# Hybrid encoder layer on one core: the moving operand of every rounded product read from two places in turn

## The chip, the core and the metric

The kernel runs on one NeuronCore of a Trainium2 chip. The metric is device time in microseconds of one execution; the kernel before takes 2334.44 us (median of three runs, 2333.82 to 2335.02). The profile is of one execution and its times are read as spans and starts on that core. The engines are TensorE (PE, its weight loads shown apart as PEld), VectorE (DVE), ScalarE (ACT), GpSimd (POOL) and the sync engine (SP), which issues most DMA.

## The reference

One layer over 256 tokens of width 2048, in float32:

```
x += 0.5 * post(FFN1(pre(x)))                  # SwiGLU, hidden width 5504
x += post(W_o(g_A * MLA(h) + g_B * RWKV7(h)))  # h = pre(x), one wide input projection w_in
x += post(XAttn(pre(x), mem))                  # cross-attention into 256 memory tokens
x += 0.5 * post(FFN2(pre(x)))
```

Nearly all of the arithmetic is dense products of 256 tokens with weight matrices (about 420 MB of weights). The RWKV scan is done in chunks of 32 tokens, with a small inverse per chunk and head.

## The kernel before, in words

**Split products.** A float32 matrix is written as a high part rounded to the engine's fast format (`float32r`) and a rounded remainder, hi + lo. A product of two such matrices is made of products of rounded parts, accumulated in one PSUM bank. `weights` (L287) streams the weights: tiles of 128 x 1024 arrive by DMA on the SP queue (`wraw`, four buffers), ACT copies the high part (L317, `whi`), DVE subtracts to get the low part (L318, `wlo`), both into rings of three slots. A tile holds 1024/n blocks of 128 x n, where n is the width of the column cut (`_CUTS`, L1579); the host's `_tiles` (L1587) lays the weights out in DRAM in just that order.

**Two forms.** In the *channel form*, `lin_ch_steps` (L330), the weights stand still in the array and the tokens move. The activations lie as high and low halves side by side (`x[:, k]` is 2 x 256 columns), so one product of the high weights with 512 moving columns (L358) and one of the low weights with the 256 high columns (L361) make a step of 128 channels; the two halves of the PSUM tile are then copied (L367) and added (L368) into `half`, and an evacuation takes it from there. The FFN's gate and up projections, the RWKV r and k, the low-rank columns, the memory keys and the cross-attention queries go this way. With `before` (one block of FFN2, L343 and L344) the two token halves are done apart.

In the *token form*, `lin_tok_steps` (L375), the tokens stand still (two blocks of 128) and n weight columns move, with three products for each block k and token half t: hi x hi (L390), hi x lo (L391), lo x hi (L392). PSUM then holds tokens by output columns. The FFN's down projections, the query latent, the RWKV v, the gates, and all output projections go this way, mostly with n = 512, the memory values with 256, the query expansion with 384 and the key/value latent with 320. `mla_heads` (L808) does the key/value expansion by hand, six kinds of products (L825 to L832) with both forms side by side on the same tile.

**What sets the order.** Within a block the code's order is the engine's order. The RWKV scan is woven with other products by `weave` (L258): a generator of the scan's steps yields how many microseconds of other work it wants in between, and a generator of *fill* work is advanced, each step counted at a fixed price, until that is reached. A token-form step (three products) is priced at `TOK_US`, a channel-form step at twice `CH_US` (L36: 0.68 and 0.35). The fill is two blocks of the attention output, the second half of r and k, two more output blocks, and then eight gate blocks of 32 steps, 256 steps in all. The scan's wants from the moment that the gate blocks begin are 2.0; eight times 1.3 (Gram matrices); 59.0 (while DVE inverts the chunk matrices, which go to memory and back into `G` at L1161); 2.2 and 1.4; six times 2.0, 2.2 and 1.4; 2.0 and 2.2; 10.0, 4.0, 6.5 and 3.0; 5.5; 5.0 and 5.0.

Products that take unrounded float32 operands (the attention scores and values, among them L1522 and L1533, the transposes, such as L517, and the scan's small products) are written separately.

Of the kernel before, what the change touches and what calls it, by code (L numbers as in the profile page):

```python
# [18 lines left out]
P = 128  # L19
# [13 lines left out]
BEFORE = 6  # L33
LEAD = 100
FIRST = 1000000
TOK_US, CH_US = 0.68, 0.35  # L36

COLS = {}

# [43 lines left out]
class Passage:  # L83
# [93 lines left out]
class Layer:  # L177
# [109 lines left out]
    def weights(self, w, nk, c0, n, feed=None, still=False, parts=False):  # L287
# [3 lines left out]
        for k in range(0, nk, kt):  # L291
# [11 lines left out]
            for j, stop in zip(cuts, cuts[1:]):  # L303
# [19 lines left out]
                for i in range(j, j + step):  # L323
                    yield k + i, hi[:, i * n : (i + 1) * n], lo[:, i * n : (i + 1) * n]

    def lin_ch(self, *args):
        for _ in self.lin_ch_steps(*args):
            pass

    def lin_ch_steps(self, w, nk, c0, n, x, evac, feed=None, before=0, parts=False, spare=False):  # L330


        nc = self.nc
        nt = n // P
        pool, tag = (self.pst, "tr") if spare else (self.psm, "mm")
        ps = [pool.tile([P, 2, T], F32, tag=tag, name="mm") for _ in range(nt)]
        held = []

        def one(t, k, hi, lo):
            ts = slice(t * P, (t + 1) * P)  # L340
            for j in range(nt):
                s = slice(j * P, (j + 1) * P)
                nc.tensor.matmul(ps[j][:, :, ts], hi[:, s], x[:, k, :, ts], start=(t + k == 0), stop=False)  # L343
                nc.tensor.matmul(ps[j][:, :, ts], lo[:, s], x[:, k, :, ts], start=False, stop=False)  # L344

        for k, hi, lo in self.weights(w, nk, c0, n, feed, True, parts):
            if k < before:
                held.append((k, hi, lo))
                one(0, k, hi, lo)
                yield k  # L350
                if k == before - 1:
                    for h in held:
                        one(1, *h)
                    yield k
                continue
            for j in range(nt):
                s = slice(j * P, (j + 1) * P)
                both = lambda: nc.tensor.matmul(ps[j], hi[:, s], x[:, k], start=(k == 0), stop=(k == nk - 1))  # L358
                if k < nk - 1:
                    both()  # L360
                nc.tensor.matmul(ps[j][:, 0, :], lo[:, s], x[:, k, 0], start=False, stop=False)  # L361
                if k == nk - 1:
                    both()
            yield k
        for j in range(nt):
            y = self.tmp.tile([P, T], F32, tag="half", name="half", bufs=2)
            nc.scalar.copy(out=y, in_=ps[j][:, 1, :])  # L367
            nc.vector.tensor_add(y, y, ps[j][:, 0, :])  # L368
            evac(j, y)

    def lin_tok(self, *args):
# [3 lines left out]
    def lin_tok_steps(self, w, nk, c0, n, xh, xl, evac, skew=0, passage=None, before=0):  # L375

        nc = self.nc  # L380
        if passage is not None:
            extra = (nk - skew + 1) // 2 * 2
            self.extra = {extra: passage.slots[0], extra + 2: passage.slots[1]}
        ps = [self.psm.tile([P, n], F32, tag="mm", name="mm") for _ in range(NT)]

        def part(x, t, k):
            return x[t][:, k, :] if isinstance(x, list) else x[:, k, t * P : (t + 1) * P]

        def step(t, k, hi, lo, first=0, last=nk - 1):
            nc.tensor.matmul(ps[t], part(xh, t, k), hi, start=(k == first), stop=False)  # L390
            nc.tensor.matmul(ps[t], part(xh, t, k), lo, start=False, stop=False)  # L391
            self.last_mm = nc.tensor.matmul(ps[t], part(xl, t, k), hi, start=False, stop=(k == last))  # L392

        held = []
        for k, hi, lo in self.weights(w, nk, c0, n):
            if k < before:
                held.append((k, hi, lo))
                step(0, *held[-1])
                yield k
                if k == before - 1:  # L400
                    for h in held:
                        step(1, *h)
                        yield k
                    held = []
                continue
            if k >= nk - skew:
                if passage is not None and not held:
                    passage.enter()
                held.append((k, hi, lo))
                if passage is not None:  # L410
                    step(0, *held[-1])
                continue
            for t in range(NT):
                step(t, k, hi, lo)
                yield k
        if passage is not None:
# [391 lines left out]
    def mla_heads(self, pool):  # L808
        nc, a = self.nc, self.a
# [5 lines left out]
        for c in range(4):  # L815
            psk = [self.psm.tile([P, T], F32, tag="mm", name="mm") for _ in range(2)]
            psv = [self.psm.tile([P, T], F32, tag="mm", name="mm") for _ in range(2)]
            for k, hi, lo in self.weights(a["w_ukv"], 2, c * 512, 512):
                kh, kl = self.ckh, self.ckl
                hv = hi.rearrange("p (h x c) -> p h x c", h=2, x=2)[:, :, 1, :]  # L820
                lv = lo.rearrange("p (h x c) -> p h x c", h=2, x=2)[:, :, 1, :]
                first, last = k == 0, k == 1
                for j in range(2):
                    s = slice(j * 256, j * 256 + P)
                    nc.tensor.matmul(psk[j], hi[:, s], kh[:, k, :], start=first, stop=False)  # L825
                    nc.tensor.matmul(psk[j], hi[:, s], kl[:, k, :], start=False, stop=False)
                    nc.tensor.matmul(psk[j], lo[:, s], kh[:, k, :], start=False, stop=last)
                for t in range(NT):
                    s = slice(t * P, (t + 1) * P)
                    nc.tensor.matmul(psv[t], kh[:, k, s], hv, start=first, stop=False)  # L830
                    nc.tensor.matmul(psv[t], kh[:, k, s], lv, start=False, stop=False)
                    nc.tensor.matmul(psv[t], kl[:, k, s], hv, start=False, stop=last)  # L832
            for j in range(2):
                nc.scalar.copy(out=self.knT[:, 2 * c + j, :], in_=psk[j])
                nc.scalar.copy(out=self.mv[:, j, c * 256 : (c + 1) * 256], in_=psv[j])
            if c == 1:
                self.do_later()

# [719 lines left out]
def layer(ctx: ExitStack, tc, a):  # L1558
# [28 lines left out]
def _tiles(w, cuts):  # L1587
# [4 lines left out]
    for n in cuts:  # L1592
        kt = WT // n
        for k in range(0, nk, kt):
            out.append(w[k * P : (k + kt) * P, c0 : c0 + n].reshape(-1, P, n).transpose(1, 0, 2).reshape(-1))
        c0 += n
    assert c0 == w.shape[1]
    return np.concatenate(out)


def _layout(inputs):
    f = lambda n: np.ascontiguousarray(np.asarray(inputs[n]))
    arr = {"x": f("x")[0], "mem": f("mem")[0], "positions": f("positions")[0].reshape(NT, P).T}
# [40 lines left out]
```

## Time and profile before

| | |
|---|---|
| median of three runs | 2334.44 us |
| span of the profiled execution | 2333.1 us |
| around the span, against the median | 1.3 us |
| TensorE busy | 2314.2 us |
| VectorE busy | 1465.1 us |
| ScalarE busy | 1136.7 us |
| DMA moved | 449.27 MB, mean 193 GB/s |
| mean granted TensorE clock | 0.998 |

A group's row reads: line, engine, operation, tile written and tiles read, array rows and columns, shape, count, then busy time and the mean duration of one, then the idle time of the engine ahead of it with what ended it. A timeline row reads: start, duration, engine, line, operation. A source row gives the shortest, median and longest duration in ns, then the first and last start. Durations of products overlap: the next one starts while the one before still drains, so the pace is read from starts.

### The profile page before, as it was taken

The numbers are of one execution on the slowest core, as the hardware profiler recorded it, in microseconds if no ns is written. First come the engines' busy times: TensorE is split into PE (matmuls) and PEld (weight loads), VectorE is DVE, ScalarE is ACT, GpSimd is POOL, SyncE is SP. The second block draws the span as 40 slices with busy tenths as digits, with TensorE's granted clock in tenths as the row PEclk, the third lists the DMA queues.
The fourth block names the chain that finished last, engine by engine and source line by source line (L and its number), as shares of the span: only waits on it lengthen the run. The fifth ranks groups of instructions, "written<-read, shape, count | busy, mean of one in ns | idle before, by whom it ended". The sixth has DMA issues, their size and how long they took to land.

```text
span 2333.1 us, 34972 instructions
## 1 busy us (share of the span) xinstructions
PE 2314.2 (99%) x13664; PEld 1984.1 (85%) x13664; DVE 1465.1 (63%) x2137; ACT 1136.7 (49%) x1670; POOL 76.3 (3%) x127
## 2 busy tenths in 40 slices
PE   9999999999999999999999999999999999999997
PEld 8888888888888888888777889888888888888886
DVE  7666666654447677768567766557666666664444
ACT  6445444544446566544334555446544544444442
POOL 0000000000000101000131000000000000000000
PEclk9999999999999999999999999999999999999999
DMA  7655555566666664545657765445555555566664
GB/s 251 208 201 190 189 190 190 189 199 198 198 198 214 210 194 152 166 148 176 212 174 243 267 200 181 169 160 172 188 190 191 190 190 191 190 200 197 198 192 144
DMA packets 137670, 449.27 MB, mean 193 GB/s; under 512 B 24096, under 2 KB 25504, under 8 KB 137248
## 3 DMA queue, kind: packets, MB, share of 16 engines
q1 hardware_dynamic: 131696, 431.94, 56.8%
q0 software_dynamic: 4944, 14.69, 2.0%
q8 instruction: 107, 1.75, 0.3%
q10 hardware_dynamic: 864, 0.40, 0.1%
q14 instruction: 59, 0.48, 0.1%
HBM read 436.48 MB, written 10.49 MB: 192 GB/s over the span
## 4 chain that ended last, share of the span: by engine, by line
PE 94%; issue 2%; DVE 2%; DMA 1%; ACT 1%; POOL 0%; SPq 0%; DVEq 0%; ACTq 0%; POOLq 0%
PE mm L358 31%; PE mm L361 16%; PE mm L390 14%; PE mm L391 14%; PE mm L392 14%; DVE wlo L318 1%; PE gr L1118 0%; PE po L1189 0%; PE po L1233 0%; PE pu L1214 0%; PE tr L494 0%; PE pn L1223 0%; PE po L1204 0%; PE bt L1122 0%; DVE X L600 0%
## 5 line engine op out<-in xcount | busy, mean ns | idle before, releaser
L318 DVE TENSOR_TENSOR wlo<-wraw,whi 128x1024 fp32r<-128x1024 f32 (+3 forms) x792 | 954.4, 1207 | 709.8 <-ACT whi L317 697.1
L317 ACT CAST whi<-wraw 128x1024 fp32r<-128x1024 f32 (+3 forms) x792 | 820.1, 1036 | 881.1 <-PE mm L392 454.8
L358 PE MATMUL mm<-hT,whi 128*128 128x512 f32 x3280 | 1140.0, 394 | 0.5 <-DVE hT L485 0.5
L361 PE MATMUL mm<-hT,wlo 128*128 128x256 f32 x3280 | 909.2, 283 | 0.5 <-DVE wlo L318 0.5
L358 PEld LDWEIGHTS mm<-hT,whi 128*128 128x128 f32 x3280 | 610.5, 188 | 126.2 <-ACT whi L317 0.8
L361 PEld LDWEIGHTS mm<-hT,wlo 128*128 128x128 f32 x3280 | 619.2, 189 | 10.1 <-DVE wlo L318 1.3
L392 PE MATMUL mm<-whi,ml 128*128 128x512 f32 x680 | 264.9, 390 | 0.0
L390 PE MATMUL mm<-whi,mh 128*128 128x512 f32 x680 | 264.8, 389 | 0.0
L391 PE MATMUL mm<-wlo,mh 128*128 128x512 f32 x680 | 264.8, 389 | 0.0
L390 PE MATMUL mm<-whi,hT 128*128 128x512 f32 (+2 forms) x512 | 188.7, 369 | 0.2 <-ACT hT L484 0.2
L391 PE MATMUL mm<-wlo,hT 128*128 128x512 f32 (+2 forms) x512 | 184.7, 361 | 1.7 <-DVE wlo L318 1.7
L392 PE MATMUL mm<-whi,hT 128*128 128x512 f32 (+2 forms) x512 | 183.9, 359 | 0.2 <-DVE hT L485 0.2
L392 PEld LDWEIGHTS mm<-whi,ml 128*128 128x128 f32 x680 | 127.7, 188 | 26.6
L390 PEld LDWEIGHTS mm<-whi,mh 128*128 128x128 f32 x680 | 127.7, 188 | 26.4
L391 PEld LDWEIGHTS mm<-wlo,mh 128*128 128x128 f32 x680 | 127.7, 188 | 26.2
L367 ACT COPY half<-mm 128x256 f32<-128x256 f32 x206 | 75.2, 366 | 134.1 <-PE mm L358 134.1
L368 DVE TENSOR_TENSOR half<-half,mm 128x256 f32<-128x256 f32 x206 | 86.1, 418 | 53.4 <-ACT half L367 53.3
L391 PEld LDWEIGHTS mm<-wlo,hT 128*128 128x128 f32 x512 | 96.4, 188 | 16.4 <-DVE wlo L318 3.3
L390 PEld LDWEIGHTS mm<-whi,hT 128*128 128x128 f32 x512 | 96.3, 188 | 15.8 <-ACT hT L484 0.5
L392 PEld LDWEIGHTS mm<-whi,hT 128*128 128x128 f32 x512 | 96.4, 188 | 14.8 <-DVE hT L485 0.8
L449 POOL TENSOR_TENSOR rstd<-rstd,mhalf 128x1 f32<-128x1 f32 x22 | 14.4, 665 | 1787.7 <-DVE rstd L447 1787.7
L390 PE MATMUL mm<-whi,mT 128*128 128x512 f32 x128 | 50.1, 391 | 0.0
(304 smaller groups left out, 1788.6 us busy)
## 6 DMA issues: line engine op xcount, KB each, us to landing
wraw<-in_w_ffn_up SPq DMA_DIRECT2D x171, 512.0 KB, 3.5
wraw<-in_w_ffn_gate SPq DMA_DIRECT2D x170, 512.0 KB, 3.5
wraw<-in_w_ffn_down SPq DMA_DIRECT2D x168, 512.0 KB, 4.2
wraw<-in_w_in SPq DMA_DIRECT2D x124, 512.0 KB, 3.6
wraw<-in_w_o SPq DMA_DIRECT2D x32, 512.0 KB, 4.2
wraw<-in_w_ckv SPq DMA_DIRECT2D x32, 512.0 KB, 3.4
wraw<-in_w_oa SPq DMA_DIRECT2D x16, 512.0 KB, 3.6
wraw<-in_w_ob SPq DMA_DIRECT2D x16, 512.0 KB, 4.3
```

The lines of the kernel that those rows point to most:

```text
L317: cast = nc.scalar.copy(out=hi[:, e], in_=raw[:, e])
L318: self.last_split = nc.vector.tensor_sub(out=lo[:, e], in0=raw[:, e], in1=hi[:, e].bitcast(F32))
L358: both = lambda: nc.tensor.matmul(ps[j], hi[:, s], x[:, k], start=(k == 0), stop=(k == nk - 1))
L361: nc.tensor.matmul(ps[j][:, 0, :], lo[:, s], x[:, k, 0], start=False, stop=False)
L367: nc.scalar.copy(out=y, in_=ps[j][:, 1, :])
L368: nc.vector.tensor_add(y, y, ps[j][:, 0, :])
L390: nc.tensor.matmul(ps[t], part(xh, t, k), hi, start=(k == first), stop=False)
L391: nc.tensor.matmul(ps[t], part(xh, t, k), lo, start=False, stop=False)
L392: self.last_mm = nc.tensor.matmul(ps[t], part(xl, t, k), hi, start=False, stop=(k == last))
L449: nc.gpsimd.tensor_tensor(out=r, in0=r, in1=self.mhalf, op=ALU.pow)
```

## The change

Every rounded product reads its moving operand as pairs, one column from the first half and one from the second half of a stretch.

- Token form: the host stores the columns of each cut wider than 256 (and the value half of the memory projection) with the even ones first and the odd ones behind them. `paired` reads column i and column i + n/2 in turn, so the output in PSUM has the plain order, and the evacuations stay.
- Channel form: nothing is stored otherwise; `woven` reads token i and token i + 64 of each block of 128 in turn. The output in PSUM has that order, and `plain` undoes it where L367 and L368 evacuate.
- The key/value expansion reads the value columns of its two heads in turn, the tokens as above, and undoes both in its copies.
- The planner's prices are 0.65 and 0.33.

The weight loads into the array, the counts of products and of columns, the DMA sizes and the order of the code stay.

```diff
-TOK_US, CH_US = 0.68, 0.35
+TOK_US, CH_US = 0.65, 0.33
...
+    def paired(self, x):
+        return x.rearrange("p (u i) -> p i u", u=2)
+    def woven(self, x):
+        if len(x.shape) == 2:
+            return x.rearrange("p (t u i) -> p t i u", u=2, i=64)
+        return x.rearrange("p a (t u i) -> p (a t) i u", u=2, i=64)
+    def plain(self, ps, y):
+        return (ps.rearrange("p (t i u) -> p t u i", u=2, i=64), y.rearrange("p (t u i) -> p t u i", u=2, i=64))
...
-                both = lambda: nc.tensor.matmul(ps[j], hi[:, s], x[:, k], start=(k == 0), stop=(k == nk - 1))
+                both = lambda: nc.tensor.matmul(
+                    ps[j], hi[:, s], self.woven(x[:, k]), start=(k == 0), stop=(k == nk - 1))
...
-                nc.tensor.matmul(ps[j][:, 0, :], lo[:, s], x[:, k, 0], start=False, stop=False)
+                nc.tensor.matmul(ps[j][:, 0, :], lo[:, s], self.woven(x[:, k, 0]), start=False, stop=False)
...
-            nc.scalar.copy(out=y, in_=ps[j][:, 1, :])
-            nc.vector.tensor_add(y, y, ps[j][:, 0, :])
+            low, tokens = self.plain(ps[j][:, 1, :], y)
+            high, _ = self.plain(ps[j][:, 0, :], y)
+            nc.scalar.copy(out=tokens, in_=low)
+            nc.vector.tensor_add(tokens, tokens, high)
...
         def step(t, k, hi, lo, first=0, last=nk - 1):
+            hi, lo = self.paired(hi), self.paired(lo)
...
-                hv = hi.rearrange("p (h x c) -> p h x c", h=2, x=2)[:, :, 1, :]
+                hv = hi.rearrange("p (h x c) -> p x c h", h=2, x=2)[:, 1]
...
+                    xh, xl = self.woven(kh[:, k, :]), self.woven(kl[:, k, :])
...
+_MOVING = {"w_ukv": lambda i, m: False, "w_ckv": lambda i, m: i % 2 == 1}
...
+        order = np.arange(n).reshape(-1, 2).T.reshape(-1) if moving(i, n) else np.arange(n)
...
-        arr[n] = _tiles(arr[n], cuts)
+        arr[n] = _tiles(arr[n], cuts, _MOVING.get(n, lambda i, m: m > 256))
```

More of the change, by code (lines that the diff above doesn't have):

```diff
@@ L342, in one @@
                 s = slice(j * P, (j + 1) * P)
-                nc.tensor.matmul(ps[j][:, :, ts], hi[:, s], x[:, k, :, ts], start=(t + k == 0), stop=False)
-                nc.tensor.matmul(ps[j][:, :, ts], lo[:, s], x[:, k, :, ts], start=False, stop=False)
+                xs = self.woven(x[:, k, :, ts])
+                nc.tensor.matmul(ps[j][:, :, ts], hi[:, s], xs, start=(t + k == 0), stop=False)
+                nc.tensor.matmul(ps[j][:, :, ts], lo[:, s], xs, start=False, stop=False)
         for k, hi, lo in self.weights(w, nk, c0, n, feed, True, parts):
@@ L819, in mla_heads @@
                 kh, kl = self.ckh, self.ckl
-                hv = hi.rearrange("p (h x c) -> p h x c", h=2, x=2)[:, :, 1, :]
-                lv = lo.rearrange("p (h x c) -> p h x c", h=2, x=2)[:, :, 1, :]
+                hv = hi.rearrange("p (h x c) -> p x c h", h=2, x=2)[:, 1]
+                lv = lo.rearrange("p (h x c) -> p x c h", h=2, x=2)[:, 1]
                 first, last = k == 0, k == 1
@@ L824, in mla_heads @@
                     s = slice(j * 256, j * 256 + P)
-                    nc.tensor.matmul(psk[j], hi[:, s], kh[:, k, :], start=first, stop=False)
-                    nc.tensor.matmul(psk[j], hi[:, s], kl[:, k, :], start=False, stop=False)
-                    nc.tensor.matmul(psk[j], lo[:, s], kh[:, k, :], start=False, stop=last)
+                    xh, xl = self.woven(kh[:, k, :]), self.woven(kl[:, k, :])
+                    nc.tensor.matmul(psk[j], hi[:, s], xh, start=first, stop=False)
+                    nc.tensor.matmul(psk[j], hi[:, s], xl, start=False, stop=False)
+                    nc.tensor.matmul(psk[j], lo[:, s], xh, start=False, stop=last)
                 for t in range(NT):
@@ L833, in mla_heads @@
             for j in range(2):
-                nc.scalar.copy(out=self.knT[:, 2 * c + j, :], in_=psk[j])
-                nc.scalar.copy(out=self.mv[:, j, c * 256 : (c + 1) * 256], in_=psv[j])
+                keys, tokens = self.plain(psk[j], self.knT[:, 2 * c + j, :])
+                nc.scalar.copy(out=tokens, in_=keys)
+                nc.scalar.copy(
+                    out=self.mv[:, j, c * 256 : (c + 1) * 256].rearrange("p (h c) -> p h c", h=2),
+                    in_=psv[j].rearrange("p (c h) -> p h c", h=2))
             if c == 1:
@@ L1583, with _tiles @@
 }
+_MOVING = {"w_ukv": lambda i, m: False, "w_ckv": lambda i, m: i % 2 == 1}
 _ROWS = ("n_ffn1_post", "n_mix_post", "n_x_post", "n_ffn2_post", "b_gate", "lnx_w", "lnx_b")
-def _tiles(w, cuts):
+def _tiles(w, cuts, moving):
     nk, out, c0 = w.shape[0] // P, [], 0
@@ L1591, in _tiles @@
         cuts = [cuts] * (w.shape[1] // cuts) + [w.shape[1] % cuts] * (w.shape[1] % cuts > 0)
-    for n in cuts:
+    for i, n in enumerate(cuts):
         kt = WT // n
+        order = np.arange(n).reshape(-1, 2).T.reshape(-1) if moving(i, n) else np.arange(n)
         for k in range(0, nk, kt):
-            out.append(w[k * P : (k + kt) * P, c0 : c0 + n].reshape(-1, P, n).transpose(1, 0, 2).reshape(-1))
+            out.append(w[k * P : (k + kt) * P, c0 + order].reshape(-1, P, n).transpose(1, 0, 2).reshape(-1))
         c0 += n
```

## The prediction

> **What bounds the kernel now.** I read the page first: busy times, the slices, the chain.
>
> ```profile
> span 2333.1 us, 34972 instructions
> PE 2314.2 (99%) x13664; PEld 1984.1 (85%) x13664; DVE 1465.1 (63%) x2137; ACT 1136.7 (49%) x1670; POOL 76.3 (3%) x127
> ...
> PEclk9999999999999999999999999999999999999999
> DMA  7655555566666664545657765445555555566664
> ...
> PE 94%; issue 2%; DVE 2%; DMA 1%; ACT 1%; POOL 0%; SPq 0%; DVEq 0%; ACTq 0%; POOLq 0%
> ...
> L358 PE MATMUL mm<-hT,whi 128*128 128x512 f32 x3280 | 1140.0, 394 | 0.5 <-DVE hT L485 0.5
> L361 PE MATMUL mm<-hT,wlo 128*128 128x256 f32 x3280 | 909.2, 283 | 0.5 <-DVE wlo L318 0.5
> ```
>
> TensorE is busy 99% of the span and is 94% of the chain, at the full granted clock, with half a microsecond of waiting before 3,280 products of a kind. Busy time of overlapping products says nothing of their pace, so I read starts from the timeline. First a run of token-form products (lines 390 to 392, 512 moving columns), then two channel-form ones (lines 358 and 361, 512 and 256 columns in turn), then runs of 320 and of 256 columns.
>
> ```profile
> 619.79 0.39 PE L392 MATMUL mm<-whi,ml 128*128 128x512 f32 x1
> ...
> 625.91 0.39 PE L392 MATMUL mm<-whi,ml 128*128 128x512 f32 x1
> ```
> ```profile
> 299.88 0.39 PE L358 MATMUL mm<-hT,whi 128*128 128x512 f32 x1
> ...
> 305.78 0.39 PE L358 MATMUL mm<-hT,whi 128*128 128x512 f32 x1
> ```
> ```profile
> 757.04 0.31 PE L390 MATMUL mm<-whi,hT 128*128 128x320 f32 x1
> ...
> 758.80 0.31 PE L390 MATMUL mm<-whi,hT 128*128 128x320 f32 x1
> ```
> ```profile
> 1419.77 0.28 PE L390 MATMUL mm<-whi,hT 128*128 128x256 f32 x1
> ...
> 1422.66 0.28 PE L390 MATMUL mm<-whi,hT 128*128 128x256 f32 x1
> ```
>
> There are 27 intervals in the first, so 6.12/27 = 226.7 ns from start to start; 17 pairs in the second, 5.90/17 = 347.1 ns; 12 in the third, 1.76/12 = 146.7 ns; 24 in the fourth, 2.89/24 = 120.4 ns. From 320 to 512 columns the pace grows by 80.0 ns over 192 columns: 0.4167 ns a column. What is left is an **offset** that does not grow with the columns: 226.7 - 213.3 = 13.4 ns at 512, 13.3 at 320, 13.7 at 256, and (347.1 - 320.0)/2 = 13.5 in the pair.
>
> Products of operands that are not rounded (plain float32) are the comparison. Merged rows give the first start and the last end, and the group rows the duration of one.
>
> ```profile
> 1496.07 1.89 PE L1522 MATMUL xsc<-kT,q 128*128 128x256 f32 x8
> ...
> 1446.81 1.04 PE L517 MATMUL tr<-ident,X 128*128 128x128 f32 x8
> ```
> ```profile
> L1522 PE MATMUL xsc<-kT,q x32: 377/379/380, 1496.1 to 1555.0; 128*128 128x256 f32 x32
> L1522 PEld LDWEIGHTS xsc<-kT,q x32: 187/190/191, 1495.8 to 1554.7; 128*128 128x128 f32 x32
> L343 PE MATMUL mm<-hT,whi x32: 277/282/365, 1601.7 to 1612.2; 128*128 128x256 f32 x32
> ```
> ```profile
> L517 PE MATMUL tr<-ident,X 128*128 128x128 f32 x32 | 4.2, 275 | 0.0
> ```
>
> (1.89 - 0.379)/7 = 215.9 ns for 256 columns, (1.04 - 0.275)/7 = 109.3 ns for 128: 0.833 ns a column, twice the rounded product's, and an offset of 215.9 - 213.3 = 2.6 ns. So an unrounded product fills the array for as long as a rounded one of 512 columns (213.3 ns), loads the same 128x128 weights (190 ns against 188), and still starts its successor 10.8 ns sooner. The two differ in how often a new column is fetched: every 0.42 ns, or every 0.83.
>
> [...]
>
> **The change, part by part.** (1) Every rounded product reads its moving operand alternately from two places: i and i + n/2 of a weight row stored permuted, or i and i + 64 of a token block. The instructions, their number, their columns and their weight loads stay. The number of them: 3,280 twice, and 1,536 at each of lines 390 to 392, of which these are the rows of line 390:
>
> ```profile
> L390 PE MATMUL mm<-whi,mh x680: 388/389/393, 486.1 to 2319.7; 128*128 128x512 f32 x170
> ...
> L390 PE MATMUL mm<-whi,hT x512: 280/389/796, 720.8 to 1553.1; 128*128 128x512 f32 x117, 128*128 128x256 f32 x43, 128*128 128x320 f32 x11
> ...
> L390 PE MATMUL mm<-whi,mT x128: 388/389/486, 1312.2 to 1400.7; 128*128 128x512 f32 x128
> ...
> L390 PE MATMUL mm<-whi,oT x120: 388/390/577, 915.7 to 1597.8; 128*128 128x512 f32 x120
> ```
>
> With 64 of the RWKV output and 32 of the query projection (from the code: 4 x 8 x 2, 4 x 4 x 2) that is 1,536, three times 4,608; with line 343's 32 and line 344's 32, and 96 of lines 825 to 832 (6 lines by 16), 6,560 + 4,608 + 64 + 96 = 11,328 products.
>
> No product in the trace alternates, so the new offset is bounded. From below nothing: 0 ns, 13.4 ns saved each, 151.8 us. From above, no bound of the same sign: the unrounded row's 0.833 ns a column is the slowest pace that the trace shows for a stream, and 4.79 million rounded columns (3,280 x 768, 4,032 x 512, 576 of 256 to 384 and 160 of 256) at 0.4167 ns more are 1,996 us. Between such far ends I take the row that it is nearest to. In turn from two places, each place is asked for its next column every 0.83 ns, as line 1522 asks its one place; that row's offset is 2.6 ns. I choose 3.0, because a product that opens two places has one first fetch more. Saved: 13.4 - 3.0 = 10.4 ns, 117.8 us over 11,328.
>
> (2) Not all of it arrives. In the opening the loads set the pace; the last stretch has hardly a product:
>
> ```profile
> 0.00:30.00 30.00, 27.86 (x141) 23.85 (x142) 20.65 (x35) 22.23 (x38) 0.73 (x7) 1.00 0.83 283
> 30.00:495.00 465.00, 465.00 (x2676) 409.70 (x2675) 305.06 (x431) 231.87 (x343) 2.06 (x2) 1.00 0.60 196
> ...
> 1260.00:1400.00 140.00, 140.00 (x634) 114.79 (x633) 93.18 (x118) 71.60 (x94) 4.38 (x7) 1.00 0.70 233
> ...
> 2320.00:2333.00 13.00, 0.58 (x3) 0.16 (x1) 6.01 (x9) 1.41 (x3) 2.72 (x2) 0.62 0.44 162
> ```
>
> The 141 products up to 30 us, with the DMA at 283 GB/s, gain nothing: 1.5 us back. Elsewhere DVE (columns after span: PE, PEld, DVE, ACT, POOL) has 305 of 465 us, the DMA at most 0.70, so 5% more demand a microsecond fits: no term.
>
> (3) Evacuation. The copy and the add of a channel-form product, 206 of each, now read PSUM two columns apart.
>
> ```profile
> L367 ACT COPY half<-mm 128x256 f32<-128x256 f32 x206 | 75.2, 366 | 134.1 <-PE mm L358 134.1
> L368 DVE TENSOR_TENSOR half<-half,mm 128x256 f32<-128x256 f32 x206 | 86.1, 418 | 53.4 <-ACT half L367 53.3
> ```
>
> From the same to double the duration: 0 to 75 us of ACT, 0 to 86 of DVE, hidden by the next block's products (four PSUM buffers, two a block) as long as DVE's 63% leaves room. Without the cover, at the few block ends that a softmax waits for, 0.8 us each; I put 1 us. The 16 copies of lines 834 and 835 go with them.
>
> (4) The planner's step prices go from 0.68 to 0.65 and from 0.35 to 0.33. The old ones equal the rows (3 x 226.7 = 680, 347); the new ones are claims, not measurements. Their effect: the chain's wants after the gate blocks begin, each rounded up to whole steps, take 241 of the 256 gate steps at 0.68 and 255 at 0.65. The fill lasts, just. The 59 us for the inverse become 91 steps, not 87: 59.2 us either way, but one weight split (4 steps, 1.2 us of DVE) more inside it.
>
> ```profile
> L1161 SPq DMA_DIRECT2D G<-td x8: 303/478/488, 1117.0 to 1120.6; - x8
> ...
> DMA to landing us min/median/max: 1.8/2.4/4.9
> ```
> ```profile
> L1214 PE MATMUL pu<-rhs,G x256: 213/214/239, 1120.2 to 1213.1; 32*32 32x64 f32 x128
> ```
>
> The first inverse lands at 1117.0 + 2.4 = 1119.4, its first use starts at 1120.2: 0.8 us spare, so at most 0.4 us of new wait there. No term.
>
> **Sum.** The profiled execution's span is 2333.1, and 1.3 us lie between it and the median of 2334.4. 2333.1 - 117.8 + 1.5 + 1.0 = 2217.8, with 1.3 around it 2219; rounded to **2218 us**. Own range: offset 2.6 and no losses, 2334.4 - 122.3 = 2212; offset 5 and 5 us of waits at block changes, 2334.4 - 95.2 + 7.5 = 2247; below that, a third of the way to the 0 ns bound (2334.4 - 151.8 = 2182.6), 2203: so 2203 to 2247.
>
> **The rivals.** *No change.* The offset may belong to the change of weights between products, in a way that only rounded products show, and the order of reading is then beside the point: 2334 us. For it: it is the same at 256, 320 and 512 columns, as a cost of each start would be. Against it: line 1522 changes its weights just as often.
>
> [...]
>
> *Slower.* The place is the read of the moving operand itself: every column now leaves the neighbourhood of the one before, and the address takes a new turn every two columns. If each turn loses one 0.4167 ns slot, 4.79 million / 2 turns are 998 us, less the 118 saved: 3,214 us; a slot for each column gives 2334 + 1996 - 118 = 4,212. It decides from 25 lost slots a product (10.4/0.4167), one in 20 columns of 512, where the saving is gone. For it: no row shows an alternating stream at this rate. Against it: line 343, whose moving operand is two runs of 128, has 282 ns against line 361's 283; its one break costs nothing visible, but one is not 255.
>
> [...]
>
> *Half of it.* The two forms stand at different distances, 256 bytes for tokens and 512 to 1,024 for most weights; if only one distance works, it is 6,624 x 10.4 = 68.9 us (2265) or 4,608 x 10.4 = 47.9 (2286).
>
> **How the numbers follow.** Forecast 0.73, half 0.08, no change 0.09, slower 0.10. The forecast's own range and the half case hold about 0.8, so the range is 2203 to 2288; the slower case, whose price is hundreds of microseconds, stays outside. Less than 0.2% (4.7 us) can't be told from no change: faster 0.81, same 0.09, slower 0.10.
>
> **What would show it.** Line 392 at 215.9 to 218 ns from start to start, the pair at 325 to 328 ns, line 1522 still at 215.9; lines 367 and 368 up to double, with nobody waiting. Starts that grow with the columns (more than 0.42 ns each) mean the slower case; an offset of 13 the unchanged one. I am wrong if the pace falls and the span does not follow: then DVE or the loads have become the bound, to be seen as idle time of TensorE behind line 318.

## The result and the profile after

The kernel with the change takes 2236.37 us (median of four, 2234.76 to 2237.75) against 2334.73 (four, 2333.82 to 2337.69): a ratio of 0.9577, 95% interval [0.9563, 0.9591], 98.4 us less. The forecast was 2218, the range 2203 to 2288.

First the page of the changed kernel: the span, the busy times, the chain, then the two groups of channel-form products and the two of their evacuation.

```profile
span 2236.0 us, 34978 instructions
PE 2206.6 (99%) x13664; PEld 1968.1 (88%) x13664; DVE 1463.7 (65%) x2137; ACT 1133.9 (51%) x1670; POOL 76.3 (3%) x127
...
PE 88%; DVE 5%; issue 4%; DMA 1%; ACT 1%; POOL 0%; DVEq 0%; ACTq 0%; SPq 0%; POOLq 0%
...
L373 PE MATMUL mm<-hT,whi 128*128 128x512 f32 x3280 | 1078.6, 383 | 0.5 <-ACT whi L317 0.5
L377 PE MATMUL mm<-hT,wlo 128*128 128x256 f32 x3280 | 882.2, 274 | 1.1 <-DVE wlo L318 1.1
...
L385 ACT COPY half<-mm 128x256 f32<-128x256 f32 x206 | 75.6, 368 | 120.4 <-PE mm L373 120.4
...
L386 DVE TENSOR_TENSOR half<-half,mm 128x256 f32<-128x256 f32 x206 | 86.1, 419 | 40.9 <-ACT half L385 40.9
```

The same 13,664 products stand in a span 97.1 us shorter. TensorE's share of the chain fell from 94% to 88%: something else now ends the work more often than before. The evacuation reads PSUM two columns apart in the time it took to read it straight (368 and 419 ns, before 366 and 418).

Then the pace, from starts in the timeline: a run of token-form products (now lines 409 to 411, 512 columns), a run of channel-form ones (lines 373 and 377), and the unrounded product that stood as the comparison.

```profile
600.21 0.38 PE L411 MATMUL mm<-whi,ml 128*128 128x512 f32 x1
...
605.39 0.38 PE L411 MATMUL mm<-whi,ml 128*128 128x512 f32 x1
```
```profile
299.77 0.38 PE L373 MATMUL mm<-hT,whi 128*128 128x512 f32 x1
...
305.99 0.38 PE L373 MATMUL mm<-hT,whi 128*128 128x512 f32 x1
...
1440.44 1.89 PE L1545 MATMUL xsc<-kT,q 128*128 128x256 f32 x8
```

Between the first two starts lie 24 products: 5.18/24 = 215.8 ns from start to start, before 226.7. Between the next two lie 19 pairs: 6.22/19 = 327.4 ns, before 347.1. The unrounded product kept its 1.89 us for eight. At 384 and 320 columns the median start to start is 162.7 and 135.8 ns, at 256 in the token form 111.7. The part that does not grow with the columns is thus 2.5 to 2.7 ns at 320, 384 and 512 columns in the token form, 5.0 at 256, and (327.4 - 320.0)/2 = 3.7 in the channel form.

Saved by the pace: 4,032 products of 512 columns x 10.8 ns = 43.5 us, 3,280 pairs x 19.6 (the mean over all pairs) = 64.3, 384 of line 409's family at 256 columns x 8.7 = 3.3, and some 3.1 for the 320, the 384 and those of line 343's form: 114.2 us. The span lost 97.1. **17 us of pace did not arrive.**

To find them, compare stage by stage, each from its first product to the first one of the next. FFN1's gate and up projections gained 26.1 us, FFN2's 26.3, the two down projections 11.2 each: within 1 us of what the pace gives (27.0, 27.3 and 11.2). Between the mixing stage and FFN2 14.8 of 16.7 arrived. The mixing stage (from the first products with `w_in` to the last gate blocks) did not: the same work lies between 720.8 and 1265.3 before, 544.5 us, and between 683.5 and 1220.2 after, 536.7 us, a gain of 7.8. Here it is cut in three, before and then after; the columns behind the two times are PE, PEld, DVE, ACT and POOL busy, the granted clock, the DMA share and GB/s.

```profile
720.80:1030.90 310.10, 308.37 (x1706) 264.27 (x1704) 227.01 (x469) 183.30 (x329) 24.80 (x41) 1.00 0.56 183
1030.90:1217.20 186.30, 186.30 (x2271) 151.47 (x2271) 120.57 (x186) 71.34 (x88) 24.34 (x43) 1.00 0.57 178
1217.20:1265.30 48.10, 47.20 (x213) 37.64 (x208) 36.15 (x47) 20.09 (x23) 11.76 (x16) 1.00 0.77 246
```
```profile
683.50:990.70 307.20, 298.42 (x1713) 261.96 (x1712) 226.39 (x470) 183.09 (x330) 24.79 (x41) 1.00 0.56 185
990.70:1184.50 193.80, 190.44 (x2305) 158.53 (x2304) 125.61 (x190) 74.95 (x93) 25.56 (x45) 0.99 0.58 183
```

TensorE stands idle for 1.7 + 0.9 = 2.6 us before (span less busy), and for 8.8 + 3.4 = 12.2 after, and in the second stretch its clock is no longer full (0.99). The share of the span did not show it: 99% both times. Neither DVE (226 of 307 us) nor the DMA (0.56) is full where the idle time arises, so the mean load does not explain it. The view of waits says what TensorE stood for, before and then after (total, times, longest):

```profile
PE mm L391 <- DVE wlo L318: 1.7, 3, 0.9
```
```profile
PE mm L410 <- DVE wlo L318: 5.1, 7, 1.8
PE mm L409 <- ACT whi L317: 1.6, 1, 1.6
...
PE tr L513 <- ACT hn L771: 1.3, 2, 0.9
...
PE mm L377 <- DVE wlo L318: 1.1, 1, 1.1
PE po L1256 <- DVE uv L1240: 0.6, 1, 0.6
```

All the rows of this view add up to 6.0 us before and 14.4 after. The two longest stops are new, and each is a queue behind a waiting instruction. In the timeline around 770 us, and then the same instruction in the profile of after_old_prices (below):

```profile
770.41 0.69 DVE L1002 TENSOR_TENSOR vp<-vp,vc 128x512 f32<-128x512 f32 x1 [2.06 <-DMA vp<-vraw]
...
771.62 1.22 DVE L318 TENSOR_TENSOR wlo<-wraw,whi 128x1024 fp32r<-128x1024 f32 x1
...
772.90 0.48 PE L410 MATMUL mm<-wlo,hT 128*128 128x512 f32 x1 [1.83 <-DVE wlo L318]
```
```profile
767.86 1.31 DVE L1002 TENSOR_TENSOR vp<-vp,vc 128x512 f32<-128x512 f32 x2 [2.95 <-DMA vp<-vraw]
```

DVE waits for the shifted RWKV rows to come back from memory (L1002); the weight split of L318 stands behind it in DVE's order, and TensorE needs that split. In the profile before, the longest wait of TensorE for a weight split was 0.9 us, and none stood at this place. That shorter products cover less of the round trip is likely one cause; the round trip itself is the other. The second transfer took 5.0 us here (issued at 765.42, used at 770.41). In after_old_prices, whose products come in the same order up to 886 us, the second transfer had landed by the time DVE was done with the first, and TensorE stood 0.41 us; in old_prices_again 0.43, in after_again 2.05. The kernel before with other prices (before_new_prices), its products as long as ever, stood 0.86 us there. So the size of this stop is in part chance.

The other stop is where the chain waits for the inverse, at 1082 us:

```profile
1081.13 1.08 PE L1237 MATMUL pu<-rhs,G 32*32 32x64 f32 x32
1082.24 0.58 ACT L1240 COPY uv<-pu 32x512 f32<-32x512 f32 x1 [7.73 <-PE pu L1237]
1082.73 2.93 ACT L317 CAST whi<-wraw 128x1024 fp32r<-128x1024 f32 x3
1083.82 0.48 PE L409 MATMUL mm<-whi,hT 128*128 128x512 f32 x1 [1.60 <-ACT whi L317]
...
1085.08 0.48 PE L410 MATMUL mm<-wlo,hT 128*128 128x512 f32 x1 [0.78 <-DVE wlo L318]
...
1086.68 0.63 PE L409 MATMUL mm<-whi,hT 128*128 128x512 f32 x1
```

The same copy before:

```profile
1121.31 0.58 ACT L1217 COPY uv<-pu 32x512 f32<-32x512 f32 x1 [0.96 <-PE pu L1214]
```

ACT's copy L1240 waits 7.73 us for the first product with the inverse, where it waited 0.96 before; three weight casts stand behind it. TensorE runs out of cast weights, stands 1.60 and 0.78 us, and then its products take 0.63 us instead of 0.38 and start every 0.43 us instead of 0.216: the granted clock is 0.50 from 1086.0 to 1088.0, for 3.41 us in all by the trace's clock records. At half the clock these cost some 1.7 us (half their length, an estimate).

### The profile page after: what moved, and what is told of

Read it like the earlier page. It is cut to its first block, busy times and chain, and to the rows that moved or that the text cites. A ratio compares the mean times of both kernels' runs of the same rounds, so it can differ in the third digit from the quotient of the medians.

```text
span 2236.0 us, 34978 instructions
## 1 busy us (share of the span) xinstructions
PE 2206.6 (99%) x13664; PEld 1968.1 (88%) x13664; DVE 1463.7 (65%) x2137; ACT 1133.9 (51%) x1670; POOL 76.3 (3%) x127
## 4 chain that ended last, share of the span: by engine, by line
PE 88%; DVE 5%; issue 4%; DMA 1%; ACT 1%; POOL 0%; DVEq 0%; ACTq 0%; SPq 0%; POOLq 0%
PE mm L373 31%; PE mm L377 15%; PE mm L409 12%; PE mm L411 12%; PE mm L410 12%; DVE wlo L318 2%; ACT whi L317 1%; DVE X L619 0%; DMA vp<-vraw 0%; DVE tm L1176 0%; PE gr L1141 0%; PE po L1256 0%; DVE TT L1179 0%; PE tr L513 0%; PE pn L1246 0%
## 5 line engine op out<-in xcount | busy, mean ns | idle before, releaser
L318 DVE TENSOR_TENSOR wlo<-wraw,whi 128x1024 fp32r<-128x1024 f32 (+3 forms) x792 | 953.9, 1207 | 620.7 <-ACT whi L317 609.1
L373 PE MATMUL mm<-hT,whi 128*128 128x512 f32 x3280 | 1078.6, 383 | 0.5 <-ACT whi L317 0.5
L377 PE MATMUL mm<-hT,wlo 128*128 128x256 f32 x3280 | 882.2, 274 | 1.1 <-DVE wlo L318 1.1
L377 PEld LDWEIGHTS mm<-hT,wlo 128*128 128x128 f32 x3280 | 630.7, 192 | 8.0 <-DVE wlo L318 2.2
L409 PE MATMUL mm<-whi,mh 128*128 128x512 f32 x680 | 257.7, 379 | 0.0
L410 PE MATMUL mm<-wlo,mh 128*128 128x512 f32 x680 | 257.7, 379 | 0.0
L411 PE MATMUL mm<-whi,ml 128*128 128x512 f32 x680 | 257.7, 379 | 0.0
L409 PE MATMUL mm<-whi,hT 128*128 128x512 f32 (+2 forms) x512 | 183.3, 358 | 1.8 <-ACT whi L317 1.6
L411 PE MATMUL mm<-whi,hT 128*128 128x512 f32 (+2 forms) x512 | 179.1, 350 | 0.3 <-DVE hT L504 0.3
L409 PEld LDWEIGHTS mm<-whi,mh 128*128 128x128 f32 x680 | 128.5, 189 | 18.2
L410 PEld LDWEIGHTS mm<-wlo,mh 128*128 128x128 f32 x680 | 128.5, 189 | 18.2
L411 PEld LDWEIGHTS mm<-whi,ml 128*128 128x128 f32 x680 | 128.5, 189 | 18.2
L409 PEld LDWEIGHTS mm<-whi,hT 128*128 128x128 f32 x512 | 97.4, 190 | 13.4 <-ACT whi L317 1.8
L468 POOL TENSOR_TENSOR rstd<-rstd,mhalf 128x1 f32<-128x1 f32 x22 | 14.4, 664 | 1698.1 <-DVE rstd L466 1698.1
```

Source lines behind the costliest of these rows:

```text
L318: self.last_split = nc.vector.tensor_sub(out=lo[:, e], in0=raw[:, e], in1=hi[:, e].bitcast(F32))
L373: both = lambda: nc.tensor.matmul(ps[j], hi[:, s], self.woven(x[:, k]), start=(k == 0), stop=(k == nk - 1))
L377: nc.tensor.matmul(ps[j][:, 0, :], lo[:, s], self.woven(x[:, k, 0]), start=False, stop=False)
L468: nc.gpsimd.tensor_tensor(out=r, in0=r, in1=self.mhalf, op=ALU.pow)
```

## The experiments

Four questions: whether the two forms each bring their own part; what the new prices do; why two places help; and whether the stop at the inverse can be had back.

**The token form alone.** The channel form reads straight.

```diff
-TOK_US, CH_US = 0.65, 0.33
+TOK_US, CH_US = 0.65, 0.35
...
-                    ps[j], hi[:, s], self.woven(x[:, k]), start=(k == 0), stop=(k == nk - 1))
+                    ps[j], hi[:, s], x[:, k], start=(k == 0), stop=(k == nk - 1))
```

> Only the token form reads in turn (4,608 products); the channel form reads straight on, its price stays 0.35. Theory (each form's offset falls by its own order of reading): lines of the token form start every 215.9 ns at 512 columns as in the changed kernel, the channel pair stays at 347 ns; 4,032 x 10.9 + 576 x 9 = 49 us less than 2334.7, of which up to 8 are lost again in the mixing stage: 2286 to 2294. Rival (one form sets the pace of the other, since both share tiles of weights): the pair moves too, and the sum of the two kernels with one form each is not the change's 98 us.

Measured: 2296.14 us (the kernel before beside it: 2335.32), ratio 0.9832 [0.9817, 0.9847]: 39.2 us less, 2 us above the expected range; the profile shows the stop and the half clock at the inverse. The token products go from start to start in 216 ns, the pair still takes 347.

**The channel form alone.** The weights are stored and read straight.

```diff
-TOK_US, CH_US = 0.65, 0.33
+TOK_US, CH_US = 0.68, 0.33
...
-            hi, lo = self.paired(hi), self.paired(lo)
```

> Only the channel form reads in turn (6,560 products and the 128 of the small blocks); the token form reads straight on, weights stored as before, price 0.68. Theory: the pair of 512 and 256 columns starts every 327.5 ns instead of 347, 3,280 x 19.5 = 64 us less, some 2 to 5 of them lost: 2271 to 2276; token products stay at 226.7 ns. Rival: as with the token form alone.

Measured: 2275.54, ratio 0.9743 [0.9728, 0.9757]: 59.8 us less, the pair in 327 ns, the token product in 226.7. The two parts add up to 99.0 us, the change has 98.4. Each form brings its own, neither paces the other, and the rival that only one distance works is gone.

**The change with the old prices, and the old kernel with the new ones.**

```diff
-TOK_US, CH_US = 0.65, 0.33
+TOK_US, CH_US = 0.68, 0.35
```

> The changed kernel with the planner's old prices, 0.68 and 0.35: 87 instead of 91 steps between the start of the inverse and its first use. Theory (the missing microseconds at the inverse come from the order in which the casts stand behind the copy of its result, which the step count sets): the stop at that place moves or goes, and the time changes by 0 to 6 us either way: 2230 to 2240. Rival (the prices matter as such, a shorter cover means a longer wait): the inverse is late by 4 x 0.65 = 2.6 us more, 2239 to 2241.

Measured: 2233.70, ratio 0.9563 [0.9549, 0.9577], 2.7 us below the changed kernel.

> The kernel before with the prices 0.65 and 0.33 alone. Theory (prices only move where the fill lies): within 3 us of 2334.7. Rival (a part of the 98 us comes from the prices): 5 us or more below it.

Measured: 2339.95, ratio 1.0018 [1.0009, 1.0028]: the prices alone cost 4.6 us, more than was expected; that they bring part of the gain is refuted. The kernel before, with nothing but the new prices, shows the same stop at the inverse (timeline):

```profile
1127.44 0.57 ACT L1217 COPY uv<-pu 32x512 f32<-32x512 f32 x1 [8.11 <-PE pu L1214]
...
1129.02 0.50 PE L390 MATMUL mm<-whi,hT 128*128 128x512 f32 x1 [1.60 <-ACT whi L317]
```

At the old price, 87 fill steps lie between the inverse and its use, and ACT's order has 22 weight casts there; at 0.65, 91 steps but 20 casts; the others stand behind the copy (L1217 here). So with the new prices TensorE has more products to do before the copy comes free and fewer weights ready for them. The stretch of half clock at the inverse appears in each profile with a token price of 0.65 at a want of 59.0 (the change twice, the token form alone, the old kernel with the new prices) and in none with 0.68 there (the kernel before, the channel form alone, the change with the old prices twice).

**How the time splits, product by product.** With the old prices the 13,664 products come in the very order of the kernel before, so each one's time to the next start can be set against the same one's before. In the profile of old_prices_again (below), 26 of these times grew by more than 0.15 us, together by 10.0 us, 8.3 of it in the mixing stage; all others together shrank by 110.6. Most of the 26 are short waits that were covered before: for weight splits (lines 377 and 410), for normalised rows (L513, 0.9 us the longest), for the inverse (L1237), for the copy behind it (L1256), the rest mostly ahead of transposes. The profile of after_old_prices has 27 such growths, 8.0 us of them in the mixing stage.

**How far apart the places must be, and how often one must change.** From the changed kernel, at the old prices: in FFN1's gate and up projections the two places stand 128 to 1 columns apart, block by block; in the down projections a run of w columns is read from each place before the other's turn.

```diff
-        return x.rearrange("p a (t u i) -> p (a t) i u", u=2, i=64)
+        return x.rearrange("p a (t u i) -> p (a t) i u", u=2, i=d)
...
-        return x.rearrange("p (u i) -> p i u", u=2)
+        return x.rearrange("p (u i w) -> p i u w", u=2, w=w)
```

> The changed kernel with the old prices; in the down projections each place is left only after a run of w columns (2, 4, 8, 16 in the four blocks of FFN1, 32, 64, 128 in FFN2, and straight reading in its last block), and in FFN1's gate and up the two places of the tokens stand 128, 32, 16, 8, 4, 2 or 1 columns apart (64 elsewhere). Theory 1 (each place has to deliver only half as often, within a few columns): at w = 1 and 2, perhaps 4 (16 bytes) the start-to-start time stays at 216 ns, from some short run on it is 226.7 again; distances of 4 columns and more are all alike at 327.5 ns a pair, 1 and 2 fall back to 347. Theory 2 (two places lie in different parts of the memory, and the load of the next weights meets the stream in one of them only): long runs still help, 64 as well as 1, and some distances, not the shortest as such, help and others don't.

Measured, channel form, start to start of a pair: 327 to 328 ns at distances of 128, 64, 32, 16, 8 and 4 columns; 347 at 2, and at 1, which is the straight reading. The timeline at a distance of 4, then of 2:

```profile
319.89 0.38 PE L389 MATMUL mm<-hT,whi 128*128 128x512 f32 x1
...
322.84 0.38 PE L389 MATMUL mm<-hT,whi 128*128 128x512 f32 x1
...
379.94 0.39 PE L389 MATMUL mm<-hT,whi 128*128 128x512 f32 x1
...
382.72 0.39 PE L389 MATMUL mm<-hT,whi 128*128 128x512 f32 x1
```

That is nine pairs in 2.95 us (327.8 ns) and eight in 2.78 (347.5). Four columns are 16 bytes, two are 8: the gain is nil at 8 bytes (347.5 ns) and whole at 16 (327.8). A distance of three columns was not run. More distance brings nothing (327 to 328 ns up to 128 columns).

Token form, start to start at 512 columns: 216 ns at w = 1, but 333 at 2, 250 at 4, 243.5 at 8, 240 at 16, 236.7 at 32, and 226.7 to 226.8 at 64, 128 and straight. The timeline at w = 2:

```profile
499.97 0.50 PE L427 MATMUL mm<-whi,ml 128*128 128x512 f32 x1
...
502.97 0.50 PE L427 MATMUL mm<-whi,ml 128*128 128x512 f32 x1
```

Nine products in 3.00 us. At w = 2 each place is asked for no more columns a microsecond than at w = 1, and the product takes 117 ns longer: how often a place is asked does not decide. The turn has to come at every column. Of the two theories the first holds for the distances and fails for the runs; the second fails, since runs of 64 and 128 columns gain nothing (226.7 to 226.8 ns).

**Whether the weight load has a part in it.** From the kernel before: in FFN1's down projection the inner products load fewer token columns as the still operand (128, 96, 64 and 32 of 128, by column cut), so that for the other tokens the kernel leaves out all but the first and last blocks' sums; and FFN2's gate and up load every second column of a block, from weights stored so that these are the right ones.

```diff
+            m = P if k in (first, last) else cols
...
-            nc.tensor.matmul(ps[t], part(xh, t, k), hi, start=(k == first), stop=False)
+            nc.tensor.matmul(ps[t][:m], part(xh, t, k)[:, :m], hi, start=(k == first), stop=False)
```

> The kernel before (moving operand read straight on) with other weight loads: in FFN1's down projection the inner products load 128, 96, 64 and 32 stationary columns in its four blocks (the rows of the tokens left out keep only the first and last block of the sum), and in FFN2's gate and up every second column is loaded, from twice the stretch of memory. Theory 2 (weight loads and the stream meet in the memory): the offset of 13.4 ns shrinks with the columns loaded, to some 10, 8 and 5 ns (starts every 224, 221, 218 ns), and grows where the load covers twice the lines, the pair above 347 ns. Theory 1 (the offset is the stream's own): 226.7 ns in all four blocks and 347 in FFN2.

Measured, start to start: 226.7 ns with 128 columns, 230 with 96, 230 with 64, 232 with 32, while the load itself took 188, 161, 135 and 107 ns; the pair with every second column 351 ns on average for 347. The timeline at 32:

```profile
679.62 0.39 PE L396 MATMUL mm<-wlo,mh 128*32 128x512 f32 x1
...
683.79 0.39 PE L396 MATMUL mm<-wlo,mh 128*32 128x512 f32 x1
```

Eighteen products in 4.17 us, 231.7 ns. A load of a quarter of the columns (107 ns for 188) takes nothing off the 13.4 ns: the theory that the load meets the stream falls. Why the smaller loads cost 3 to 5 ns more stays open. The weights still change at every product here, as they do in the changed kernel, whose offset is 2.5 ns: it is the changed kernel itself that refutes the forecast's *no change* rival.

**More than two places.** From the change at the old prices: u places in turn instead of two.

```diff
-        return x.rearrange("p a (t u i) -> p (a t) i u", u=2, i=64)
+        return x.rearrange("p a (t u i) -> p (a t) i u", u=u, i=d)
```

> The changed kernel with the old prices; in FFN1's gate and up the tokens are read from 4, 8, 16, 32, 64 or 128 places in turn, 64, 32, 16, 8, 4 or 2 columns apart (9 patterns, two blocks each), and in its down projection the weight columns from 4, 16, 128 and 256 places, 128, 32, 4 and 2 columns apart. Theory 3 (only this matters, that no two columns in succession lie in the same 16 bytes): all patterns that stand 4 columns or more apart start as the changed kernel does, 327.5 ns a pair and 216 ns, however many places; the two that stand 2 apart have two columns of one 16-byte line in succession and are back at 347 and 226.7. Theory 4 (two places are what the memory path can hold open; with more, each line is fetched again for every column): from 4 or 8 places on the times rise above 347 and 226.7, growing with the columns.

Measured, the pair of the channel form: 427 ns for 4 places 64 columns apart, 404 for 4 places 4 apart, 662 for 8 places 32 apart, and 648 to 720 for 8 to 128 places otherwise. Token form, 512 columns: 283 ns for 4 places, 435 for 16, 461 for 128, 451 for 256; the unchanged two places in FFN2 215.8. The timeline at 4 places 64 apart, then at 8 places 32 apart:

```profile
69.97 0.45 PE L379 MATMUL mm<-hT,whi 128*128 128x512 f32 x1
...
73.81 0.45 PE L379 MATMUL mm<-hT,whi 128*128 128x512 f32 x1
...
200.50 0.62 PE L379 MATMUL mm<-hT,whi 128*128 128x512 f32 x1
...
203.81 0.63 PE L379 MATMUL mm<-hT,whi 128*128 128x512 f32 x1
```

Nine pairs in 3.84 us, 426.7 ns, and five in 3.31, 662. With eight places a 512-column product takes 440 ns, 2.06 times its 213.3: (440 - 213.3)/512 = 0.44 ns more a column, about one column's 0.4167 ns. Two places in turn take 327.4 ns a pair and four take 404 to 427, although each of the four is asked half as often as each of the two. The third theory falls; the fourth, two places held open at once, fits this sweep and the one of distances. It does not fit the runs of two columns, which also come from two places and cost 333 ns. What the sweeps show is where the gain is, not how the memory brings it about.

**The wait at the inverse moved.** In the change the want is raised by 0.8 us, so that two more fill steps go ahead of the copy; in the change at the old prices it is raised to 60.4.

```diff
-        yield 59.0
+        yield 59.8
```

> The changed kernel with 59.8 instead of 59.0 us wanted for the inverse: 93 steps instead of 91, and three more casts stand ahead of the copy of the result on ACT. Theory (the stop after the inverse is ACT's order: the casts of the next weights wait behind a copy that waits for TensorE, and the idle TensorE falls to half its clock): the stop of 1.8 and 1.3 us and the slow 3.4 us go, 2230 to 2233. Rival (the stop is the loads, which stand behind the inverse's transfers on SP's queue, whatever the order on ACT): it stays, 2236 to 2238.

Measured: 2237.26, ratio 0.9589 [0.9571, 0.9608], no gain. ACT at the inverse:

```profile
1079.81 1.04 ACT L317 CAST whi<-wraw 128x1024 fp32r<-128x1024 f32 x1 [5.60 <-DMA wraw<-in_w_in]
...
1084.56 0.58 ACT L1240 COPY uv<-pu 32x512 f32<-32x512 f32 x1 [1.22 <-PE pu L1237]
```

The copy no longer waits long and the clock stays full there, but now a cast waits 5.60 us for its weights: their loads stand on SP's queue behind the transfers of the inverse (issued from 1070.77 us for 4.84 us, the loads from 1075.71), and the time is the rival's. The stop at 772.9 us is there as in the changed kernel, 2.07 us for 1.83; the edit, whose order is the same up to 1080 us, has no part in it. Two stretches of half clock came, the granted clock 0.50 from 774 to 776 us, behind that stop, and again from 1184 to 1186.

> The changed kernel with the old prices and 60.4 us: 89 steps instead of 87, 57.7 us at the new pace instead of 56.4. Theory: the wait of 1.1 us ahead of the first product with the inverse goes, nothing else moves: 2231 to 2234. Rival (the inverse is not what it waits for): the wait stays, and two more gate steps before it shift the casts: 2234 to 2238.

Measured: 2236.20, ratio 0.9578 [0.9564, 0.9592], no gain either. The wait ahead of the first product with the inverse fell from 0.45 us (old_prices_again) to 0.16, and a stop of 3.15 us for a weight split, at 1188.5 us, with half the clock behind it (0.50 from 1190 to 1192), has come; one profile does not tell whether the edit brought it.

**The change and its old-price form again**, the same two kernels as above.

> The changed kernel once more, beside the next one on the same chip: 2236 to 2237.

> The changed kernel with the old prices 0.68 and 0.35 once more. Theory (the new prices cost the stop after the inverse and the slow stretch behind it): 2 to 4 us below the changed kernel of the same call. Rival (the 2.7 us were chance): within 1 us of it.

Measured: 2236.35 (ratio 0.9575 [0.9562, 0.9588]) and 2234.36 (0.9571 [0.9558, 0.9584]). The old prices are 2.0 us ahead here and 2.7 above; seven of their eight executions lie at or below 2234.56, and eight of the nine of the change above it. The intervals of the ratios overlap: some 0.1% in favour of the old prices is likely and not settled. (One difference between the profiles, the stop at 772.9 us, lies ahead of the first place where the order differs, so the prices did not make it.) That form, at 2233.7 to 2234.4, is the fastest of this study.

## Why the prediction was right, and where not

**The bound and step (1), the pace: right in size.** TensorE's start-to-start set the span, and the offset of 13.4 ns went to 2.5 in the token form and 3.7 in the channel form, where 3.0 was put (5.0 at 256 columns in the token form). The first fetch that the 3.0 added to line 1522's 2.6 was the author's estimate; no run shows one apart. 114.2 us stand against 117.8. The rows named as signs came out: line 411 at 215.8 ns, the pair at 327.4, line 1545 unchanged.

**The reason given for it: only half right.** The prediction took the offset for a matter of fetching the moving operand, and the sweeps agree: the distance decides it (347.5 ns a pair at 2 columns, 327.8 at 4) and so does the turn (216 ns at w = 1, 226.7 at 64), the load of the still operand does not (231.7 ns with a quarter of it). But "each place is asked for its next column every 0.83 ns" is not what lifts it. Runs of two columns and four places in turn ask each place as seldom or more seldom and cost 333 and 283 ns. The whole gain came only where two places, and no more, alternated at every column, 16 bytes or more apart (215.8 ns, 327.4 a pair). That the estimate from line 1522 gave the right number is luck as far as this reason goes: line 1522 reads one place straight on.

**Step (2), "so 5% more demand fits: no term": this failed.** The mean load of DVE and DMA does fit (the busy shares above), and the prediction stopped there. What the shorter products uncover are waits that do not shrink with them: a transfer's round trip in front of the weight splits in DVE's order, the latent's norm, the copy behind the inverse. With the order of before unchanged they come to 10.0 us, 8.3 of them in the mixing stage, where the pace brings 11.5 + 6.0 + 2.2 = 19.7 us (three stretches as above, growths over 0.15 us set aside) and 11.4 arrive. The sign that the prediction named for being wrong, idle time of TensorE behind line 318, shows in small: 6.2 us in the view of waits (lines 410 and 377), 2.2 before.

**Step (2), the opening: put too large.** The product that follows the 141 starts at 30.20 us before and 29.23 after, 0.97 us earlier, where the pace gives 1.2; the lead grows from 0.24 us at 17.5 us to 0.96 at 30.0. So some 0.3 us were lost, not 1.5 (the other profiles of the change are 0.5 to 1.5 us ahead there).

**Step (3), the evacuation: its lower bound.** 368 and 419 ns; the 1 us put for it was not needed.

**Step (4), the prices, "at most 0.4 us of new wait there. No term": this failed too.** The prices move work: the order of the code does not stay as it was, the products' order differs from 886 us on. The count of steps was right (91 for 87) and so was the place, but the prediction looked at TensorE's wait for the inverse alone. On ACT two casts moved behind a copy that waits for that inverse; TensorE stood 2.4 us for weights and lost some 1.7 us (half of 3.41, an estimate) to half a clock. Alone the prices cost 4.6 us [2.1 to 6.5, from the interval of the ratio]; with the change the medians lie 2.0 and 2.7 apart, which is not settled. The prediction asked what it costs to arrive early at the inverse, and not who stands behind the instruction that waits for it.

**The sum.** 2333.1 - 114.2 (pace) + 17.1 = 2236.0. Of the 17.1, TensorE's idle time accounts for (2236.0 - 2206.6) - (2333.1 - 2314.2) = 10.5, the half clock for 1.7 and the opening for 0.3 at most. The remaining 4.6 are put down to waits that don't show as idle: a product is marked busy for 0.38 us and paced at 0.216, so some 0.16 us of every wait lies under its mark. Two waits of old_prices_again show it: ahead of line 410 at 771.95 and 775.02 us the time between starts grew by 0.58 and 0.36 us, and 0.43 and 0.21 are marked idle. That the whole 4.6 is of this kind is argued, not shown. The forecast of the span, 2217.8, missed by 18.2: 3.6 in the pace, 17.1 that did not arrive, less the 1.5 and the 1.0 that the prediction had put for the opening and the evacuation. (With 1.3 us around the span its own sum is 2219, not 2218.) That the time lies within the forecast's own range, up to 2247, is partly luck: most of that room was for an offset of 5 ns, and the loss came from waits, for which 5 us were put.

**The rivals.** *Half of it*: refuted by the two forms apart. *No change*: refuted. *Slower*: products that grow so do appear, between two places (215.8 ns) and four (283); at two places, one column each, there is no such cost. Nor does the number of turns decide: a turn at every column is the fastest order of all here (215.8 ns), and runs of two, which turn half as often, take 333.

## What to carry to other kernels

Where rounded float32 products follow each other without a gap and their start-to-start stands 13 ns above the columns' time (226.7 against 213.3 here), read the moving operand column by column from two places at least 16 bytes apart (215.8 ns; at 8 bytes the pair gained nothing), and not from more than two (283 ns from four). Here the evacuation cost nothing for it (368 and 419 ns, before 366 and 418). Expect the gain to shrink where waits that do not shorten with the products had just been covered (17 of 114 us here): look, for every instruction that waits on a transfer or a chain, at what stands behind it on its engine, since a mean load with room says nothing of that. Leave a planner's prices alone until the order that they make has been looked at; a right price can give a worse order.

## What was not expected of the hardware

- The straight reading of a rounded operand costs 10.8 ns a product over the alternating one, the same at 320, 384 and 512 columns (8.7 at 256). A fetch that was too slow at every column would cost by the column. Why it is a constant stays open; no run here tells.
- Runs of two columns from each place cost 333 ns, which is 1.5 times the columns' 213.3 and the 13.4 of the straight reading; longer runs cost less and less, and from 64 columns nothing. Also open.
- Seven stretches of half the granted clock lie between stretches of full clock in the profiles here, each of 3.413 us and each costing some 1.7 us (half its length, an estimate). The length of the stop ahead does not decide alone. The stops at the inverse (1.60 us, then some 0.78) came with one each time; a single stop of 2.07 us (want_59_8, at 772.9 us) was followed by one; one of 2.05 at the same place (after_again, 772.7) and one of 2.38 (sweep_places, 830.8) were not. The longest stop marked ahead of the seven is 3.15 us (old_prices_want_60_4). What halves the clock, and why for 3.413 us each time, stays open.
